# First layer's state recurrence: two half chains, or four quarter chains with products over half of K beside the last two

## The chip, the core and the metric

One core of a Trainium2 chip runs the whole program: two layers of a decoder on a sequence of 256 positions with 2048 channels. The metric is the time of one execution in microseconds (us) of device time. An instruction is put on one of five queues (TensorE, VectorE, ScalarE, GpSimd, and SyncE, which issues most DMAs), and each queue works through its own in order.

## What is computed

```python
def s5_mixer(u, ...):                      # first layer, u is the normed input
    ...                                    # lb = exp(lam*dt), coef = (lb-1)/lam, bb = coef*b
    st = scan(lb, u @ bb)                  # st[t] = lb*st[t-1] + bu[t], complex, 64 states a group
    y = st.re @ c.re - st.im @ c.im + d_skip * u
    val, gate = split(gelu(y) @ w_glu, 2)  # w_glu: 2048 x 4096
    return val * sigmoid(gate)

x = x + s5_mixer(rmsnorm(x))
x = x + swiglu_ffn(rmsnorm(x))
x = x + dilated_attention(...)             # second layer
x = x + swiglu_ffn(rmsnorm(x))
```

There are 128 groups of 16 channels, each with 64 complex states, and only this first layer has a recurrence. Everything else is a product with a large fp32 weight matrix.

## The kernel before

**Products.** Each weight matrix comes in chunks of 1 MB (four K tiles of 128 rows by 512 columns). ScalarE rounds half a chunk to `whi`, VectorE takes the rest into `wlo`, and TensorE multiplies them with activations that are split in the same way: three matmuls for each of two K tiles and two halves of the sequence, twelve for half a chunk. `products` (L113) issues them, `feed` (L127) a whole chunk, `block` (L146) a block of 512 output columns. Three buffers hold raw chunks, three hold `whi` and three `wlo`.

**The recurrence.** The 256 positions are cut into 64 blocks of four. The states are kept for 64 pairs of groups, as `sts`; a quarter `qr` has 16 of these pairs, so a quarter of the channels, and two quarters a half. For each quarter:

- `gain` and `taps` multiply the input matrix by the first three powers of lb (`gps`),
- `taps_T` transposes four pairs' worth of it, `inject` multiplies it with the input `ub` (built by `build_u`), and ScalarE copies the result into `sts`; sixteen such injections, four to a quarter,
- `scan` (L480) carries the state from block to block, 63 steps of three VectorE operations: a product with the fourth power into PSUM and two additions,
- `build_m` (L456) makes the matrix that acts inside a block, from `cp` (`build_c`) and `gps`; ScalarE copies it to `mt` and SyncE's queue shifts it by six small DMAs,
- `y_local` multiplies the inputs by `mt`, `y_state` the states by `fds` (`powers`), both into the same banks of PSUM; `gelu` follows, and `turn` and `low` transpose the result and split it into the activations `lhs` of the products.

In `s5_glu` the instructions of TensorE, ScalarE, GpSimd and, in part, VectorE keep the order in which they are written (`InOrder`), so this order is a schedule by hand. `run` takes one operation from each of several chains in turn, `steps` does so for a number of steps. Before the change there are two chains, `sa` for the first half of the pairs and `sb` for the second, with 128 and 64 elements to an operation. `sa` starts beside the taps of quarters 2 and 3, `sb` 16 steps behind it, and then both run side by side:

```python
        steps(LEAD - 6, sa)
        ...
        for qr in range(4):
            build_m(qr)
        ...
        steps(33 - LEAD, sa, sb)
        ...
        steps(16, sa, sb)
```

When `sa` is done, the first half's gelu and turn follow, then four half chunks of gate block 4 (over the first half of K, `high`, `rest` and `feed`) beside the last steps of `sb`, then the second half's `y_state` and gelu, then the other four half chunks. All other gate and value blocks come afterwards over the whole of K, with `block`.

GpSimd has `build_c`, `d_skip` and `powers`.

## Time and profile before

| | us |
|---|---|
| three runs of the kernel before | 2425.85, 2426.14, 2428.14 |
| their median | 2426.14 |
| span of the profiled execution, first to last instruction | 2426.5 |
| share of it in which TensorE is busy | 2391.7 |
| the same for VectorE, ScalarE, GpSimd | 1323.9, 1081.6, 113.5 |
| first 120 us of it: TensorE, VectorE | 90.4, 110.3 |

The execution that was profiled has no other time than its span, so the span stands for it. In the rows of the timeline there is the start, the time that a merged row is busy, the engine, the line, the operation, the tile written and those read, the shapes, and in brackets how long the engine was idle before it and who ended that. Inside `s5_glu` nearly every instruction has the line of `InOrder` (L59), so the tile names tell them apart: `mm<-mm,actr` and `actr<-actr,mm` are the recurrence, `ms<-dsm,ident` and `ms<-cb,gp` are build_m, `tr<-actr` and `ms<-actr` are y_local, `ms<-fdx,actr` and `tr<-fdx,actr` y_state, `gm` is gelu's result, `ms<-ident,gm` the turn, `actt` the activations.

### The profile page before, as it was taken

The page shows a single profiled execution, that of the slowest core. Times are in us where ns is not written, and L with a number is a line of the kernel's source. Part 1 is how long each engine was busy: PE and PEld are TensorE (multiplying, and loading weights), DVE is VectorE, ACT ScalarE, POOL GpSimd, SP SyncE. Part 2 cuts the span into 40 slices and gives each one's busy share as a digit, 9 for nine tenths or more (in the row PEclk, how much of TensorE's full clock was granted, in tenths as well). Part 3 has the DMA queues.
Part 4 walks back from the last instruction along what each step waited for, and adds up shares of the span by engine and source line. Part 5 has one row for each costly group of instructions (what it writes and reads, how often), then busy time and mean ns, then how long its engine had stood idle before and what let it go on. Part 6 is the DMA issues. An engine that isn't in the chain of part 4 may idle for free.

```text
span 2426.5 us, 29375 instructions
## 1 busy us (share of the span) xinstructions
PE 2391.7 (99%) x11856; PEld 1934.7 (80%) x11856; DVE 1323.9 (55%) x1974; ACT 1081.6 (45%) x1367; POOL 113.5 (5%) x113
## 2 busy tenths in 40 slices
PE   6899999999999999999999999999999999999999
PEld 5788888888888888888888888888888888888887
DVE  9955454444444454555446776765454444454454
ACT  7344444444334444554445555554444433344433
POOL 4800000000000000000000000000000000000000
PEclk9899999999999999999999999999999999999999
DMA  2245555555555555555554444445555555555554
GB/s 85 90 167 177 190 183 181 191 177 187 191 184 182 189 185 180 186 188 187 178 191 164 155 152 154 156 156 186 180 189 181 184 191 188 184 184 188 178 197 148
DMA packets 63033, 423.58 MB, mean 175 GB/s; under 512 B 8112, under 2 KB 9520, under 8 KB 12336
## 3 DMA queue, kind: packets, MB, share of 16 engines
q1 hardware_dynamic: 61744, 419.60, 50.8%
q8 instruction: 93, 1.52, 0.3%
q10 hardware_dynamic: 1152, 2.10, 0.2%
q14 instruction: 44, 0.36, 0.0%
HBM read 418.79 MB, written 2.10 MB: 173 GB/s over the span
## 4 chain that ended last, share of the span: by engine, by line
PE 97%; DVE 2%; ACT 1%; issue 0%; DMA 0%; SPq 0%; DVEq 0%
PE mm L122 30%; PE mm L124 30%; PE mm L123 30%; PE ms L59 2%; PE tr L59 1%; PE ms L863 1%; PE tr L743 1%; PE mm L59 1%; PE tr L814 1%; DVE mm L59 0%; PE tr L863 0%; PE tr L185 0%; DVE gp L59 0%; DVE gpb L59 0%; PE ms L893 0%
## 5 line engine op out<-in xcount | busy, mean ns | idle before, releaser
L104 DVE TENSOR_TENSOR wlo<-raw,whi 128x1024 fp32r<-128x1024 f32 x776 | 948.6, 1224 | 1001.5 <-ACT whi L103 1000.0
L103 ACT CAST whi<-raw 128x1024 fp32r<-128x1024 f32 x776 | 813.6, 1049 | 1159.4 <-PE mm L124 1139.7
L122 PE MATMUL mm<-whi,actt 128*128 128x512 f32 x3104 | 1234.8, 398 | 0.3 <-ACT whi L103 0.3
L124 PE MATMUL mm<-whi,actt 128*128 128x512 f32 x3104 | 1228.6, 396 | 0.0
L123 PE MATMUL mm<-wlo,actt 128*128 128x512 f32 x3104 | 1228.5, 396 | 0.0
L124 PEld LDWEIGHTS mm<-whi,actt 128*128 128x128 f32 x3104 | 582.6, 188 | 139.8
L123 PEld LDWEIGHTS mm<-wlo,actt 128*128 128x128 f32 x3104 | 582.6, 188 | 137.6 <-DVE wlo L104 0.4
L122 PEld LDWEIGHTS mm<-whi,actt 128*128 128x128 f32 x3104 | 582.6, 188 | 137.4 <-ACT whi L103 0.5
L794 POOL TENSOR_TENSOR sc<-ssq,mhalf 128x8 f32<-128x8 f32 x16 | 32.1, 2005 | 474.9 <-DVE ssq L792 474.9
L174 POOL TENSOR_TENSOR r<-m,mhalf 128x1 f32<-128x1 f32 x6 | 3.2, 552 | 1053.1 <-DVE m L173 846.4
L59 DVE TENSOR_TENSOR actr<-actr,mm 128x64 f32<-128x64 f32 x252 | 46.8, 216 | 2.0
L729 ACT ACTIVATE sg<-mm,r 128x512 f32<-128x512 f32 x44 | 30.1, 688 | 21.3 <-PE mm L124 21.0
L872 ACT ACTIVATE s<-s,mx 128x384 f32<-128x384 f32 (+1 forms) x32 | 24.8, 774 | 29.1 <-DVE mx L870 29.1
L59 DVE TENSOR_TENSOR mm<-mm,actr 128x128 f32<-128x128 f32 x126 | 37.0, 294 | 0.9
L59 POOL TENSOR_TENSOR fpr<-pf,cp 128x512 f32<-128x512 f32 x32 | 34.9, 1090 | 0.0
L733 DVE SCALAR_TENSOR_TENSOR sg<-mm,r,sg 128x512 f32<-128x512 f32 x44 | 30.9, 743 | 0.0
L59 ACT COPY actr<-ms 128x252 f32<-128x252 f32 (+1 forms) x40 | 19.8, 578 | 22.5 <-PE ms L59 21.2
L790 ACT ACTIVATE sq<-mm 128x512 f32<-128x512 f32 x32 | 19.0, 593 | 23.5 <-PE mm L124 23.5
L747 DVE TENSOR_TENSOR actt<-tr,actt 128x512 fp32r<-128x512 f32 x44 | 28.2, 682 | 0.0
L877 DVE SCALAR_TENSOR_TENSOR p<-s,z,p 128x128 f32<-128x128 f32 (+1 forms) x64 | 26.4, 412 | 3.2 <-ACT p L875 3.0
L746 ACT CAST actt<-tr 128x512 fp32r<-128x512 f32 x44 | 23.6, 590 | 10.0 <-PE tr L743 10.0
L743 PE MATMUL tr<-ident,sg 128*128 128x128 f32 x176 | 26.7, 274 | 0.0
(180 smaller groups left out, 938.0 us busy)
## 6 DMA issues: line engine op xcount, KB each, us to landing
raw<-w_gu SPq DMA_DIRECT2D x176, 1024.0 KB, 4.8
raw<-w_down SPq DMA_DIRECT2D x88, 1024.0 KB, 4.8
raw<-w_q SPq DMA_DIRECT2D x48, 1024.0 KB, 4.8
raw<-w_glu SPq DMA_DIRECT2D x32, 1024.0 KB, 4.8
raw<-w_kv SPq DMA_DIRECT2D x32, 1024.0 KB, 4.8
raw<-w_o SPq DMA_DIRECT2D x16, 1024.0 KB, 4.8
actr<-x_c SPq DMA_DIRECT2D x2, 1024.0 KB, 6.1
xr<-x_t SPq DMA_DIRECT2D x8, 256.0 KB, 5.2
```

The costliest lines, as they stand in the source:

```text
L59: return lambda *a, **k: self.tc.keep_in_program_order(call(*a, **k))
L103: (scalar or self.nc.scalar).copy(out=hi, in_=r)
L104: (vector or self.nc.vector).tensor_tensor(out=lo, in0=r, in1=hi.bitcast(FP32), op=ALU.subtract)
L122: matmul(ps[th], lhsT=a[:, 0, ts], rhs=hi, start=(k == 0), stop=False)
L123: matmul(ps[th], lhsT=a[:, 0, ts], rhs=lo, start=False, stop=False)
L124: matmul(ps[th], lhsT=a[:, 1, ts], rhs=hi, start=False, stop=(k == n - 1))
L729: nc.scalar.activation(out=s, in_=ps[th], func=AF.Silu, scale=rs[th])
L733: nc.vector.scalar_tensor_tensor(out=sg[th], in0=ps[th], scalar=rs[th], in1=sg[th], op0=ALU.mult, op1=ALU.mult)
L743: nc.tensor.transpose(out=pt[:, k, th * P:(th + 1) * P], in_=sg[th][:, c:c + P], identity=self.ident)
L747: nc.vector.tensor_tensor(out=ht[:, k0:k0 + 2, 1], in0=pt, in1=ht[:, k0:k0 + 2, 0].bitcast(FP32), op=ALU.subtract)
L794: nc.gpsimd.tensor_tensor(out=sc, in0=ssq, in1=self.mhalf.rearrange("p (a b) -> p a b", a=2), op=ALU.pow)
L877: nc.vector.scalar_tensor_tensor(out=pr, in0=sc[:, g], scalar=z, in1=pr, op0=ALU.mult, op1=ALU.add)
```

## The change

There are now four chains of one quarter each, with 64 and 32 elements to an operation. The first two, `sq[0]` and `sq[1]`, run side by side to their end. Then come the first half's gelu and turn, and then 28 half chunks of products over the first half of K, for seven of the eight gate and value blocks (`HALF1`). Between them VectorE takes two, two or three steps of `sq[2]` and `sq[3]` for each half chunk (`BSTEPS`). Six of the seven blocks are copied to SBUF by ScalarE as partial sums, since two pairs of PSUM banks serve them in turn; the seventh stays in PSUM. At the end of these products the second half's gelu and turn follow. Later each of the seven is fed over the other half of K (`whole`), and VectorE adds the partial sum. The twelve products of one half chunk (two K tiles) are called a slot in the prediction.

The same diff does more. The last quarter's taps and three of the four gains go to GpSimd. Taps have 512 elements to an operation instead of 256, nine operations instead of 18. The tables of lb's powers are written straight to PSUM, and ScalarE copies them to SBUF for GpSimd (`keep`). The coefficients are made right behind lb, den's operations before it. `pair` makes both parts of a complex product at once. The input `x_c` is loaded from ScalarE's queue instead of SyncE's, and the root mean square's scaling (`rc`) moves from VectorE to ScalarE. `y_local` for quarters 0 and 1 is written between the build_m of quarters 1, 2 and 3.

```diff
-LEAD = 16
+HALF1 = (0, 5, 1, 6, 2, 7, 4)
+BSTEPS = (2, 2, 3)
...
+        for q in range(2):
+            A.dma_start(out=xc[:, 16 * q:16 * q + 16], in_=io["x_c"][:, 16 * q:16 * q + 16])
...
+        def keep(t0, t1):
+            for t in range(t0, t1):
+                A.copy(out=pf[:, t].rearrange("p k r m -> p r k m"), in_=tabs[t])
...
-        def scan(h):
-            st = sts[h]
-            f, pr = fsc[h], prs[h]
+        def scan(qr):
+            st = sts[qr // 2][:, qr % 2]
+            f, pr = fsc[qr], prs[qr]
             for c in range(63):
                 hh, v = st[:, c], st[:, c + 1]
-                yield lambda: tt(pr, f, hh.unsqueeze(1).broadcast_to([P, 2, 2, 32]), ALU.mult, W)
+                yield lambda: tt(pr, f, hh.unsqueeze(1).broadcast_to([P, 2, 2, 16]), ALU.mult, W)
...
+        coefs()
         power()
-        gain(0)
         power()
...
+        gain(0, W)
+        for qr in (1, 3, 2):
+            gain(qr, G)
+        run(taps(0))
...
+        keep(0, 3)
+        build_c(0)
+        build_c(1)
+        run(taps(3, G))
+        d_skip()
         run(taps(1))
         power()
...
+        for i in range(4):
+            g0, gtt = gtt, taps_T(i + 1)
+            inject(i, g0)
+            if i == 0:
+                keep(3, 4)
...
+        sq = [scan(qr) for qr in range(4)]
+        run(itertools.islice(sq[0], 9), taps(2))
...
+        build_m(0)
+        build_m(1)
+        steps(32, sq[0], sq[1])
+        yl = {0: y_local(0, self.ps_tr, "tr")}
+        build_m(2)
+        yl[1] = y_local(1, self.ps_mm, "mm")
+        build_m(3)
...
+        for qr in range(2):
+            y_state(qr, yl[qr], 0, 32)
...
+        steps(28, sq[0], sq[1])
+
+        slots = [(b, c, h) for b in HALF1 for c in range(2) for h in range(2)]
...
+        def feed(k):
+            i, s = divmod(k, 4)
+            if s == 0:
+                self.blk = self.open_block(KT if i == last else KT // 2, 0, banks[i % 2])
+            r, hi, lo = ws.pop(k)
+            self.products(self.blk, [(hi[:, j], lo[:, j]) for j in range(2)], lhs, T)
+            if s == 3 and i < last:
...
+                part = room[i]
+                for th in range(2):
+                    A.copy(out=part[:, th], in_=self.blk[0][th])
+                parts[HALF1[i]] = [part[:, th] for th in range(2)]
...
+        high(0)
+        high(1)
+        y_state(0, yl[0], 32, 64)
+        gms[0] = gelu(yl[0])
+        steps(3, sq[1], sq[2])
+        rest(0)
+        y_state(1, yl[1], 32, 64)
+        pts = [turn(0, j4) for j4 in range(2)]
+        gms[1] = gelu(yl[1])
+        rest(1)
+        for j4 in range(2):
+            low(0, j4, pts[j4])
+        for k in range(len(slots)):
+            if k + 2 < len(slots):
+                high(k + 2)
+            if k > 0 and k + 1 < len(slots):
+                rest(k + 1)
+            if k < len(slots) - 2:
+                steps(BSTEPS[k % len(BSTEPS)], sq[2], sq[3])
+            feed(k)
+            if k == 0:
+                for j4 in range(2):
+                    low(1, j4, turn(1, j4))
+            if k == 3:
+                yl[2] = y_local(2, self.ps_ms, "ms")
+            if k == 17:
+                y_state(2, yl[2], 0, 32)
+            if k == len(slots) - 3:
+                y_state(2, yl[2], 32, 64)
+                gms[2] = gelu(yl[2])
+                run(sq[3])
+                yl[3] = y_local(3, self.ps_mm, "mm")
+                y_state(3, yl[3], 0, 64)
+                gms[3] = gelu(yl[3])
...
+                half = self.open_block(KT, KT // 2)
+                for c in range(2, 4):
+                    self.feed(half, src[c], lhs)
+                for th in range(2):
+                    nc.vector.tensor_tensor(out=parts[b][th], in0=half[0][th], in1=parts[b][th], op=ALU.add)
+                return parts[b]
```

Three places of the order of instructions follow. The first is TensorE between the last injections and the first turn; `gp` is the taps matrix of a quarter, `fdx` the output powers. Before:

```order
L59 MATMUL ms<-cb,gp_229 128x64 x16
L59 MATMUL ms<-dsm,ident 128x16x16 x2
L59 MATMUL ms<-cb,gp_230 128x64 x16
L59 MATMUL ms<-dsm,ident 128x16x16 x2
L59 MATMUL ms<-cb,gp_231 128x64 x16
L59 MATMUL ms<-actr 64x64 x32
L59 MATMUL tr<-actr 64x64 x32
L59 MATMUL ms<-fdx,actr 32x64 x64
L59 MATMUL tr<-fdx,actr 32x64 x64
L59 MATMUL mm<-actr 64x64 x32
L59 MATMUL mm<-actr 32x64 x64
L59 MATMUL ms<-fdx,actr 32x64 x64
```

And the same place of TensorE now:

```order
L60 MATMUL ms<-cb,gp_250 128x64 x16
L60 MATMUL tr<-actr 64x64 x32
L60 MATMUL ms<-dsm,ident 128x16x16 x2
L60 MATMUL ms<-cb,gp_251 128x64 x16
L60 MATMUL mm<-actr 64x64 x32
L60 MATMUL ms<-dsm,ident 128x16x16 x2
L60 MATMUL ms<-cb,gp_252 128x64 x16
L60 MATMUL tr<-fdx,actr 32x64 x64
L60 MATMUL mm<-fdx,actr 32x64 x64
L60 MATMUL tr<-fdx,actr 32x64 x64
L60 MATMUL mm<-fdx,actr 32x64 x64
L60 MATMUL ms<-ident,gm 128x128 x8
```

The two y_local have moved ahead of the build_m of quarters 2 and 3, and the third quarter's y_local and first y_state are gone from here.

The second place is VectorE where the first weights are split; `wlo<-raw,whi` is the low half of a slot's weights. Before:

```order
L59 TENSOR_TENSOR wlo<-raw,whi 128x1024
L59 TENSOR_TENSOR mm<-mm,actr 128x128
L59 TENSOR_TENSOR actr<-actr,mm 128x64 x2
L59 TENSOR_TENSOR mm<-mm,actr 128x128
L59 TENSOR_TENSOR actr<-actr,mm 128x64 x2
L59 TENSOR_TENSOR actt<-ms,actt 128x4x64 x4
```

And now, on VectorE:

```order
L60 TENSOR_TENSOR wlo<-raw,whi 128x1024 x2
L60 TENSOR_TENSOR actt<-ms,actt 128x4x64 x4
L60 TENSOR_TENSOR mm<-mm,actr 128x64 x2
L60 TENSOR_TENSOR actr<-actr,mm 128x32 x4
L60 TENSOR_TENSOR mm<-mm,actr 128x64 x2
L60 TENSOR_TENSOR actr<-actr,mm 128x32 x4
L60 TENSOR_TENSOR actt<-ms,actt 128x4x64 x4
L60 TENSOR_TENSOR wlo<-raw,whi 128x1024
```

A lone half chain has become a pair of quarter chains, with two products and four additions to a step, and the second turn's low half stands ahead of the third slot's split.

The third place is ScalarE around the first injections; `gt<-tr` copies transposed taps, `actr<-ms` copies an injection into the states. Before:

```order
L59 COPY gt<-tr 128x512 x2
L59 COPY actr<-ms 128x2x2x63 x2
L59 COPY gt<-tr 128x512
L59 COPY actr<-ms 128x2x2x63 x2
L59 COPY gt<-tr 128x512
```

And now, on ScalarE:

```order
L60 COPY pf<-mm 128x2x2x64 x3
L60 COPY gt<-tr 128x512 x2
L60 COPY actr<-ms 128x2x2x63 x2
L60 COPY pf<-mm 128x2x2x64
L60 COPY gt<-tr 128x512
L60 COPY actr<-ms 128x2x2x63 x2
```

The copy of the fourth power's table, which VectorE makes behind the second quarter's taps, stands between the first and the second injection.

More of the change, by code (lines that the diff above doesn't have):

```diff
@@ L352, in s5_glu, with coefs @@
-        prs = [half(tbq[:, 128:256]), half(tbp[:, 128:256])]
-        def gain(qr):
+            form(k, z)
+        cf = late.tile([P, 2, 2, 64], FP32, name="cform")
+        def coefs():
+            ni = lam[:, 1]
+            stt(t1, lam[:, 0], -1.0, ca, ALU.add, ALU.mult)
+            tt(t2, ni, cb_, ALU.mult)
+            stt(t3, lam[:, 0], -1.0, cb_, ALU.add, ALU.mult)
+            tt(t4, ni, ca, ALU.mult)
+            tt(cf[:, 0, 0], t1, t2, ALU.add)
+            tt(cf[:, 0, 1], t3, t4, ALU.subtract)
+            ts(cf[:, 1, 1], cf[:, 0, 0], -1.0, None, ALU.mult)
+            V.tensor_copy(out=cf[:, 1, 0], in_=cf[:, 0, 1])
@@ L506, in powers @@
             for t in range(4):
-                for k in range(2):
-                    pair(fds[qr][:, t, k], pf[t][:, :, k, mo:mo + 16], cp[:, :, mo:mo + 16])
+                pair(fds[qr][:, t], pf[:, t, :, :, mo:mo + 16], cp[:, :, mo:mo + 16])
         def y_local(qr, pool, nm):
@@ L607, in high, with rest @@
             A.copy(out=hi, in_=r)
-            ws[c, half] = (r, hi, lo)
-        def rest(c, half):
-            r, hi, lo = ws[c, half]
+            ws[k] = (r, hi, lo)
+        def rest(k):
+            r, hi, lo = ws[k]
             tt(lo, r, hi.bitcast(FP32), ALU.subtract, W)
-        def feed(c, half):
-            r, hi, lo = ws.pop((c, half))
-            self.products(gb0, [(hi[:, k], lo[:, k]) for k in range(2)], lhs, T)
-        gtile, lhs = {}, []
+        gtile = {}
         def turn(qr, j4):
@@ L638, in low @@
                 tt(lo, pt[:, :, xx], hi.bitcast(FP32), ALU.subtract, W)
-        def turns(qr):
-            for j4 in range(2):
-                low(qr, j4, turn(qr, j4))
-        high(0, 0)
-        high(0, 1)
-        high(1, 0)
-        y_state(0, yl[0], range(8), 32, 64)
-        gms = {0: gelu(yl[0])}
-        y_state(1, yl[1], range(4), 32, 64)
-        for half in range(2):
-            steps(3, sb)
-            rest(0, half)
-        steps(2, sb)
+        banks = [[t.rearrange("p a b c -> p (a b c)") for t in yl[qr]] for qr in range(2)]
@@ L662, in s5_glu @@
-        feed(0, 0)
-        high(1, 1)
-        pts = [turn(1, j4) for j4 in range(2)]
-        feed(0, 1)
-        steps(2, sb)
-        for j4 in range(2):
-            low(1, j4, pts[j4])
-        rest(1, 1)
-        run(sb)
-        feed(1, 0)
-        high(2, 0)
-        feed(1, 1)
-        rest(2, 0)
-        y_state(2, yl[2], range(8), 32, 64)
-        high(2, 1)
-        rest(2, 1)
-        gms[2] = gelu(yl[2])
-        yl[3] = y_local(3, self.ps_mm, "mm")
-        y_state(3, yl[3])
-        turns(2)
@@ L682, in s5_glu @@
-        gms[3] = gelu(yl[3])
-        feed(2, 0)
-        high(3, 0)
-        rest(3, 0)
-        feed(2, 1)
-        high(3, 1)
-        rest(3, 1)
-        turns(3)
-        feed(3, 0)
-        feed(3, 1)
+        for k in range(len(slots)):
[20 more added lines that the diff above has]
+                gms[3] = gelu(yl[3])
+            if k == len(slots) - 2:
+                pts = [turn(2, j4) for j4 in range(2)]
+            if k == len(slots) - 1:
+                for j4 in range(2):
+                    low(2, j4, pts[j4])
+                for j4 in range(2):
+                    low(3, j4, turn(3, j4))
@@ L692, in s5_glu @@
         late.release()
+        blk = self.blk
         with tc.tile_pool(name="glu", bufs=2, reuse_waits="tile") as work:
@@ L707, in s5_glu @@
                     sg.append(s)
-                ps = self.block([io["w_glu"][nb, c] for c in range(4)], lhs)
+                ps = whole(nb)
                 for th in range(2):
@@ L715, in s5_glu @@
                 self.xT_part(nb, nxt)
-            return [l for _, l in nxt], self.stats_end(), gains
+            res = [l for _, l in nxt], self.stats_end(), gains
+        carry.release()
+        return res
     def ffn(self, layer, lhs, rs, nxt=None, out=None):
```

248 lines of the change are left out of this document (113 added, 135 removed).

## Prediction

> **What bounds the kernel now.** I read the page first, then busy time by stage, then the timeline of the first 213 us.
>
> ```profile
> span 2426.5 us, 29375 instructions
> ...
> PE 97%; DVE 2%; ACT 1%; issue 0%; DMA 0%; SPq 0%; DVEq 0%
> ```
>
> The chain of work that ended last is TensorE's for 97% of the span. So the time is the products' own, plus whatever TensorE spends before and between them, and that lies in the first layer. The trace was taken on an execution with a span of 2426.5 us; the runs' median is 2426.14, so I sum on the trace and take the difference off the median.
>
> ```profile
> 60.10:75.10 15.00, 12.62 (x95) 11.29 (x95) 14.83 (x93) 7.38 (x18) 14.37 (x18) 1.00 0.08 22
> 75.10:92.20 17.10, 16.67 (x137) 15.50 (x138) 17.10 (x112) 4.65 (x10) 16.39 (x19) 0.50 0.29 90
> 92.20:119.00 26.80, 19.12 (x760) 17.83 (x756) 23.33 (x113) 7.41 (x15) 20.17 (x21) 0.87 0.34 111
> 131.20:157.00 25.80, 24.83 (x390) 20.57 (x390) 11.00 (x14) 10.69 (x21) 0.00 (x0) 1.00 0.26 89
> ```
>
> The columns are the stage, its length, busy time of PE, weight loads, VectorE, ScalarE and GpSimd, the granted clock and DMA. Up to 119 us VectorE is the full one in most stages: it runs the recurrence. TensorE waits for it, and from 75.1 to 92.2 it is busy at half clock.
>
> ```profile
> 119.01 0.50 PE L59 MATMUL tr<-whi,actt 128*128 128x512 f32 x1 [0.96 <-ACT gm L59]
> ...
> 157.42 0.39 PE L122 MATMUL mm<-whi,actt 128*128 128x512 f32 x1
> ...
> 158.12 0.40 PE L122 MATMUL mm<-whi,actt 128*128 128x512 f32 x1
> ```
>
> The first product starts at 119.0. Three products take 0.70 us, so a half chunk (12 products, from here on a slot) takes 2.80. By 157.0 the eight slots of the hand-written stage and a third of the next are done. From there TensorE runs dense, so 28 slots are done at 157.0 + 19.67 x 2.80 = **212.1 us** (the transposes of one x block, which the changed kernel still has to do at that point, are left out). What follows is the same work in both kernels; so the question is when the changed kernel has 28 slots done.
>
> **The change, part by part.**
>
> *Front of VectorE and the injections.* The tables, taps and injections come in another order.
>
> ```profile
> 2.77 0.70 DVE L290 COPY ldt<-spp 128x64 f32<-128x64 f32 x1 [2.77 <-DMA spp<-sp]
> ...
> 12.00 0.22 DVE L243 SCALAR_TENSOR_TENSOR lam<-t,mag 128x64 f32<-128x64 f32 x1
> ...
> 14.76 0.68 DVE L59 TENSOR_TENSOR gp<-bt,gb 128x512 f32<-128x512 f32 x1
> ```
> ```profile
> actr<-x_c SPq DMA_DIRECT2D x2, 1024.0 KB, 6.1
> ```
> ```profile
> 30.62 1.04 ACT L59 COPY actr<-ms 128x252 f32<-128x252 f32 x2
> ...
> 32.23 1.07 ACT L59 COPY actr<-ms 128x252 f32<-128x252 f32 x2
> ```
> ```profile
> 37.07 2.13 ACT L59 COPY actr<-ms 128x252 f32<-128x252 f32 x4
> ...
> 46.26 1.05 ACT L59 COPY actr<-ms 128x252 f32<-128x252 f32 x2 [1.59 <-PE ms L59]
> ```
>
> lam is ready at 12.2. The six added operations for den fill gaps of a dependent chain: 0.5. x_c now goes out on ScalarE's queue beside spp, for which VectorE's first operation waits: between nothing and the 3.3 by which x_c's 6.1 is above that 2.77; I take 1.0, since spp is small. From lam at 12.00 to the first gain at 14.76 stand one table, one power and rc's operation. A second power (about half of that, 1.3) and eight small operations for the coefficients (1.0) are added, and rc's goes to ScalarE: between 4.0 and 5.1, and I take 4.4. Then come a gain, 18 tap operations of 512 elements at 0.60 (by the line through 0.20 for 128 and 1.13 for 1024 elements, rows below), 12 waits of 0.13 on the operation before, and the third power: 0.6 + 10.8 + 1.6 + 1.3. That gives 12.2 + 0.5 + 1.0 + 4.4 + 14.3 = 32.4, and keep(3, 4), which ScalarE has in its row ahead of the next injections, ends at 32.8. Everything behind it on ScalarE waits: seven rounds of 1.61, less a transposed copy at the end, 10.7 to the eighth injection; 7.1 from there to the ninth's copies (39.2 to 46.26, with build_u between); then 1.05, five rounds (8.05), a copy (0.6) and the last injection on TensorE (1.1). **S**, where build_m starts, is 61.4, against 60.2 before. taps(3) leaves VectorE for GpSimd.
>
> ```profile
> L59 POOL TENSOR_TENSOR fpr<-pf,cp 128x512 f32<-128x512 f32 x32 | 34.9, 1090 | 0.0
> ```
>
> Nine of these are 10 us. From about 15, when the coefficients are there, GpSimd has three gains, two build_c (six operations) and taps(3): 18 x 1.09, done near 35. Their first reader is the thirteenth injection, near 54; with 19 us of cover the move costs nothing there, and VectorE is rid of 6 us. Behind it stand d_skip, powers(0), two build_c and powers(1), 32 operations more: near 70, and the first reader of powers(1) comes at 88 (below).
>
> *TensorE from S to the first product.*
>
> ```profile
> 60.16 1.10 PE L59 MATMUL ms<-dsm,ident 128*128 128x256 f32 x4
> 61.87 3.79 PE L59 MATMUL ms<-cb,gp 128*128 128x64 f32 x32 [0.60 <-ACT cb L59]
> 65.49 1.08 PE L59 MATMUL ms<-dsm,ident 128*128 128x256 f32 x4
> ...
> 71.05 1.08 PE L59 MATMUL ms<-dsm,ident 128*128 128x256 f32 x4
> ...
> 79.87 7.09 PE L59 MATMUL ms<-cb,gp 128*128 128x64 f32 x32
> 86.89 0.48 PE L59 MATMUL ms<-actr 128*64 128x64 f32 x4
> ```
> ```profile
> 91.06 2.59 PE L59 MATMUL tr<-actr 128*64 128x64 f32 x64
> 93.58 2.62 PE L59 MATMUL ms<-fdx,actr 64*32 64x64 f32 x126
> ```
> ```profile
> 131.28 9.73 PE L59 MATMUL mm<-actr 64*32 64x64 f32 x320
> ```
> ```profile
> 87.42 3.68 SPq L477 DMA_DIRECT2D actr<-actr  x6
> ```
> ```profile
> actr<-actr SPq DMA_DIRECT2D x8, 48.0 KB, 2.0
> ```
>
> At full clock the first two build_m take 5.33 and 5.56. y_local(0), now directly behind them, waits for the six shift copies of build_m(0) (issue 3.68, landing 2.0): about 1.0. It takes 2.6, and so does y_local(1); build_m(2) and (3) find their operands ready behind these, 4.9 each. Four half y_state at 2.65 are 10.6. Sum 37.5.
>
> ```profile
> 115.04 1.09 PE L59 MATMUL ms<-ident,gm 128*128 128x128 f32 x8
> 115.73 2.10 ACT L59 CAST actt<-ms 128x256 fp32r<-128x256 f32 x4 [0.47 <-PE ms L59]
> ...
> 116.89 2.24 DVE L59 TENSOR_TENSOR actt<-ms,actt 128x256 fp32r<-128x256 f32 x4 [2.68 <-ACT actt L59]
> ```
>
> From turn to the first low half are 2.4 us, in which two products already fit: 1.9. So the first product runs at S + 39.4 = **100.8 + h**, where h is what half clock costs. Here it cost 26.7 for four build_m (60.16 to 86.89) where the sum above has 20.7 to 22: about 5. Its bounds are 0 and, with all four build_m at 7.09 plus twice 1.08, 16 and more. I take 5, from the same work one rearrangement away. The Trainium skill's page TensorE: Matmul & The Clock Gate (Why this matters for your kernels) asks for an idle gap above about 3 us before the clock falls; by it h is 0. The trace disagrees: 16.67 of 17.10 us busy, clock 0.50.
>
> *VectorE: is the first half's recurrence ready by then?*
>
> ```profile
> 62.45 0.29 DVE L59 TENSOR_TENSOR mm<-mm,actr 128x128 f32<-128x128 f32 x1
> 62.65 0.35 DVE L59 TENSOR_TENSOR actr<-actr,mm 128x64 f32<-128x64 f32 x2
> 62.91 0.29 DVE L59 TENSOR_TENSOR mm<-mm,actr 128x128 f32<-128x128 f32 x1
> ```
> ```profile
> 53.38 0.30 DVE L59 TENSOR_TENSOR mm<-mm,actr 128x128 f32<-128x128 f32 x1
> 53.72 0.47 DVE L59 TENSOR_TENSOR actr<-actr,mm 128x64 f32<-128x64 f32 x2
> 54.23 0.30 DVE L59 TENSOR_TENSOR mm<-mm,actr 128x128 f32<-128x128 f32 x1
> ```
> ```profile
> 120.61 1.22 DVE L59 TENSOR_TENSOR wlo<-raw,whi 128x1024 fp32r<-128x1024 f32 x1
> 121.74 0.29 DVE L59 TENSOR_TENSOR mm<-mm,actr 128x128 f32<-128x128 f32 x1
> ```
>
> Two half chains side by side take 0.46 per step each, a lone one 0.85: 0.20 (128 elements) or 0.13 (64) until the next operation issues, 0.13 more until one that needs the result. A quarter's operations have 64 and 32 elements, 0.13 and 0.10. A pair's step is then 0.67 by issue and 0.72 by dependence: p = 0.73 (bounds 0.67, and 0.93 if size bought nothing). The scan starts when the fourth injection is in, three rounds behind 32.8, near 38. It runs 6.4 beside taps(2), and then 63 pair steps, 46: done at 90. TensorE asks at S + 34.8 = 96.2. Cover 6 us: the recurrence is off the path up to p = 0.82.
>
> *The loop.* 28 x 2.80 = 78.4. On TensorE between them: turn(1) 1.1, y_local(2) 2.6, y_state(2) 5.3, y_local(3) and y_state(3) 2.6 + 4.5 (9.73 less a local and a half state), turns 2.2, waits 0.5, and a wait at the third slot: VectorE splits its weights only after low(1), which ends some 2.9 behind turn(1) (115.04 + 1.09 to 116.89 + 2.24), so at 6.8 behind the first product, and the split at 8.0, where TensorE asks at 6.7; 1.2. In all 20.0. VectorE has 1.13 + 7/3 x 0.73 = 2.83 per slot against 2.80, hidden by the 7.9 of state work between. The partial sums (12 copies on ScalarE, 12 additions on VectorE) lie under products; they lengthen the way to three x blocks a little, 0.6. End: 100.8 + 98.4 + 0.6 = 199.8 + h. Against 212.1 the gain is 12.3 - h, so 7.3, and the forecast is **2419.0 us**.
>
> **Rivals.** *The clock stays full* (h = 0): 2413.8. For it: the new order is denser, and the two y_local break up the build_m. Against it: the row at 0.50. Chance 0.27; the clock page named above would give this one. *Small operations cost what large ones do* (p = 0.93): the first half's recurrence ends at 44.4 + 63 x 0.93 = 103, the first product is at 107.5 (a half y_state and 1.9 behind it), and in the loop VectorE needs 1.13 + 2.17 = 3.30 per slot. The tables in PSUM that y_local(3) overwrites are then free 8.0 + 24 x 1.13 + 58 x 0.93 + 2.5 = 91.5 behind the first product, where TensorE asks after 83.0 (26 slots are 72.8; turn(1), y_local(2), y_state(2) and the wait at the third slot are 10.2). So 107.5 + 98.4 + 8.5 + 0.6 = 215.0, or 2429. Against it: 0.20 and 0.13 for 128 and 64 elements. It eats the whole gain from p = 0.90 on. Chance 0.12. *Half clock from S to the first product*, the one on the slow side: four build_m at 9.25 are 16 more, the local and state products some 6 more, so 22 against a gain of 12.3: 2436. It decides from 17 us of loss on, which is nearly the whole stage of 39 us at half clock. For it: these matmuls did run at 0.50 while busy. Against it: in this stage the clock was back after 17.1 us. Chance 0.06. *Several small waits* that no row here shows eat most of the gain: 2424, chance 0.10. The DMA page of the Trainium skill (DMA: Bandwidth & Descriptors, Queues, rings and completion order) has engines take turns between queues by packet, which would make spp later than my 1.0; no run here shows it.
>
> **Numbers.** The forecast has 0.45. About 0.2% (4.9 us) can be told from no change. Faster: 0.40 of the forecast and the full clock, 0.67; slower: the half-clock rival and half of p = 0.93, with a remainder, 0.13; within, 0.20. Range 2412 to 2428: below it 0.04, above it 0.16.
>
> **What would show it.** Right: first product at 100 to 107, busy TensorE from build_m on, pair steps of 0.7 to 0.75, VectorE idle before the first product, 28 slots done by about 205. Wrong: TensorE waiting for VectorE ahead of y_state, wlo ahead of the products in most slots, or a clock of 0.50 over more than 17 us.

## The result, and the profile after

The changed kernel takes 2452.51 us (median of 4 runs, 2451.01 to 2453.20), the kernel before 2426.32 beside it: ratio 1.0107, 95% interval 1.0093 to 1.0122. It is 26 us slower, where 7.3 us faster was forecast, and lies outside the range. The profiled execution took 2451.01. One execution of a later kernel, e4_before_one, took 11396.57 and is left out of its time and ratio.

The page of the changed kernel: the span, and the chain of work that ended last.

```profile
span 2449.2 us, 29727 instructions
...
PE 91%; DVE 8%; issue 1%; ACT 0%; DMA 0%; DVEq 0%
...
L60 DVE TENSOR_TENSOR actr<-actr,mm 128x32 f32<-128x32 f32 x504 | 64.6, 184 | 8.0 <-ACT actr L60 3.5
L60 DVE TENSOR_TENSOR mm<-mm,actr 128x64 f32<-128x64 f32 x252 | 58.3, 231 | 8.1 <-ACT pf L60 0.4
```

Before, 97% of that chain was TensorE's; now 8% of it is VectorE's. The two groups are the recurrence. An operation on a quarter is hardly shorter than one on a half: 0.23 against 0.29 for a product, 0.18 against 0.22 for a sum, and there are twice as many.

TensorE's timeline ahead of the first product:

```profile
68.86 1.10 PE L60 MATMUL ms<-dsm,ident 128*128 128x256 f32 x4
...
98.53 1.64 PE L60 MATMUL mm<-fdx,actr 64*32 64x64 f32 x91 [1.80 <-issue]
114.77 3.45 PE L60 MATMUL tr<-fdx,actr 64*32 64x64 f32 x128 [14.60 <-DVE actr L60]
118.05 2.24 PE L60 MATMUL mm<-fdx,actr 64*32 64x64 f32 x128
...
121.58 0.50 PE L60 MATMUL tr<-whi,actt 128*128 128x512 f32 x1 [0.26 <-ACT actt L60]
```

TensorE has its first half states at 100.2 and then stands 14.60 us for the recurrence. This is VectorE in that wait, and later in the loop:

```profile
107.32 0.50 DVE L60 TENSOR_TENSOR mm<-mm,actr 128x64 f32<-128x64 f32 x2
107.85 0.51 DVE L60 TENSOR_TENSOR actr<-actr,mm 128x32 f32<-128x32 f32 x4
108.39 0.50 DVE L60 TENSOR_TENSOR mm<-mm,actr 128x64 f32<-128x64 f32 x2
...
128.97 1.22 DVE L60 TENSOR_TENSOR wlo<-raw,whi 128x1024 fp32r<-128x1024 f32 x1
...
132.14 1.22 DVE L60 TENSOR_TENSOR wlo<-raw,whi 128x1024 fp32r<-128x1024 f32 x1
...
136.38 1.22 DVE L60 TENSOR_TENSOR wlo<-raw,whi 128x1024 fp32r<-128x1024 f32 x1
```

Two products and four sums are a pair step: from 107.32 to 108.39 it is **1.07**, against the 0.73 of the forecast. GpSimd is idle by then. In the loop a slot with two pair steps takes VectorE 3.17 and one with three 4.24, so 3.53 on average, against TensorE's 2.80. Counted by the products' records, the 28th slot is done at 233.2, before at 213.1; that is 20.1 of the 22.7 by which the spans of the two traces differ.

### The profile page after: what moved, and what is told of

Its sections match the earlier page's. It is cut to its first block, busy times and chain, and to the rows that moved or that the text cites. A ratio compares the mean times of both kernels' runs of the same rounds, so it can differ in the third digit from the quotient of the medians.

```text
span 2449.2 us, 29727 instructions
## 1 busy us (share of the span) xinstructions
PE 2385.8 (97%) x11856; PEld 1925.3 (79%) x11856; DVE 1377.0 (56%) x2309; ACT 1088.8 (44%) x1384; POOL 122.7 (5%) x105
## 4 chain that ended last, share of the span: by engine, by line
PE 91%; DVE 8%; issue 1%; ACT 0%; DMA 0%; DVEq 0%
PE mm L123 29%; PE mm L124 29%; PE mm L125 29%; DVE mm L60 3%; DVE actr L60 2%; DVE wlo L60 1%; PE ms L898 1%; PE tr L778 1%; PE tr L849 1%; PE tr L898 0%; PE tr L186 0%; PE tr L60 0%; PE mm L60 0%; DVE gp L60 0%; PE ms L60 0%
## 5 line engine op out<-in xcount | busy, mean ns | idle before, releaser
L105 DVE TENSOR_TENSOR wlo<-raw,whi 128x1024 fp32r<-128x1024 f32 x756 | 924.3, 1224 | 967.2 <-ACT whi L104 965.8
L104 ACT CAST whi<-raw 128x1024 fp32r<-128x1024 f32 x756 | 792.8, 1049 | 1125.7 <-PE mm L125 1102.0
L123 PE MATMUL mm<-whi,actt 128*128 128x512 f32 x3008 | 1196.8, 398 | 0.0
L124 PE MATMUL mm<-wlo,actt 128*128 128x512 f32 x3008 | 1190.9, 396 | 0.0
L125 PE MATMUL mm<-whi,actt 128*128 128x512 f32 x3008 | 1190.8, 396 | 0.0
L125 PEld LDWEIGHTS mm<-whi,actt 128*128 128x128 f32 x3008 | 564.7, 188 | 135.1
L123 PEld LDWEIGHTS mm<-whi,actt 128*128 128x128 f32 x3008 | 564.7, 188 | 132.9
L124 PEld LDWEIGHTS mm<-wlo,actt 128*128 128x128 f32 x3008 | 564.7, 188 | 132.5
L60 DVE TENSOR_TENSOR actr<-actr,mm 128x32 f32<-128x32 f32 x504 | 64.6, 184 | 8.0 <-ACT actr L60 3.5
L60 DVE TENSOR_TENSOR mm<-mm,actr 128x64 f32<-128x64 f32 x252 | 58.3, 231 | 8.1 <-ACT pf L60 0.4
L60 ACT CAST whi<-raw 128x1024 fp32r<-128x1024 f32 x28 | 29.4, 1052 | 41.6 <-PE tr L60 21.0
L60 PE MATMUL tr<-whi,actt 128*128 128x512 f32 x128 | 42.1, 400 | 0.6 <-DVE actt L60 0.4
L60 DVE TENSOR_TENSOR wlo<-raw,whi 128x1024 fp32r<-128x1024 f32 x28 | 34.1, 1221 | 0.0
L60 PE MATMUL tr<-wlo,actt 128*128 128x512 f32 x64 | 26.3, 412 | 5.2 <-DVE wlo L60 4.6
L60 PE MATMUL mm<-whi,actt 128*128 128x512 f32 x96 | 30.7, 396 | 0.0
```

Of the source, the lines that this page charges most:

```text
L60: return lambda *a, **k: self.tc.keep_in_program_order(call(*a, **k))
L104: (scalar or self.nc.scalar).copy(out=hi, in_=r)
L105: (vector or self.nc.vector).tensor_tensor(out=lo, in0=r, in1=hi.bitcast(FP32), op=ALU.subtract)
L123: matmul(ps[th], lhsT=a[:, 0, ts], rhs=hi, start=(k == k0), stop=False)
L124: matmul(ps[th], lhsT=a[:, 0, ts], rhs=lo, start=False, stop=False)
L125: matmul(ps[th], lhsT=a[:, 1, ts], rhs=hi, start=False, stop=(k == n - 1))
```

## The experiments

Two questions: why the pair step takes 1.08 (theory A: the chains wait for each other; theory B: small operations are slow), and where the front lost its 7 us. All ratios are to the kernel before, run beside it; a range in brackets is the 95% interval.

**e1_apart.** The products of the two chains in different PSUM tiles, and the chains one operation apart.

```diff
...
-        prs = [half(tb2[:, 256 + 64 * k:320 + 64 * k], 16) for k in range(4)]
+        prs = [half((tb2, tb3)[k % 2][:, 256 + 64 * k:320 + 64 * k], 16) for k in range(4)]
...
-        run(itertools.islice(sq[0], 9), taps(2))
+        run(itertools.islice(sq[0], 10), taps(2))
...
+        run(itertools.islice(sq[2], 1))
         steps(3, sq[1], sq[2])
```

The lines left out here give tb3 room for these products and change nothing else.

> The changed kernel, with the products of the odd quarters' chains in another PSUM bank than those of the even ones, and the second chain of a pair one operation behind the first. In the changed kernel a pair step of two quarter chains took 1.08 us where 0.73 was forecast. Theory A (the pair is slow because its two products lie in one PSUM tile, so that each chain's product waits until the other chain has written or read its own): with two tiles only the waits inside a chain are left, 0.267 behind a product and 0.221 behind a sum, and by issue and dependence the pair step becomes 0.74. The first half's recurrence, which has some 60 pair steps from 50 us on, ends near 95 in place of 114.8, TensorE (done with the first half states at 100.2) no longer waits, the first product starts near 107, a half chunk costs VectorE 1.13 + 7/3 x 0.74 = 2.86, 28 slots are done near 206 in place of 233.2, and the time is near 2425. Theory B (operations of 64 and 32 elements are slow by themselves, by a fixed cost or because their factor is read in runs of 16): the pair step stays at 1.08 and the time within 3 us of 2452.5.

Measured 2427.94, ratio 1.0007 (0.9998 to 1.0016): 24.6 us come back. VectorE's timeline of this run, at the same work:

```profile
71.10 0.23 DVE L60 TENSOR_TENSOR mm<-mm,actr 128x64 f32<-128x64 f32 x1
71.24 0.31 DVE L60 TENSOR_TENSOR actr<-actr,mm 128x32 f32<-128x32 f32 x2
71.47 0.23 DVE L60 TENSOR_TENSOR mm<-mm,actr 128x64 f32<-128x64 f32 x1
71.60 0.32 DVE L60 TENSOR_TENSOR actr<-actr,mm 128x32 f32<-128x32 f32 x2
71.83 0.23 DVE L60 TENSOR_TENSOR mm<-mm,actr 128x64 f32<-128x64 f32 x1
```

From 71.10 to 71.83 is a pair step: 0.73, with operations of the same length as in the changed kernel (0.23 and 0.18). So it was not their size. The loop from first product to 28th slot takes 97.0 in place of 111.6. The first product starts at 117.0, though, not at 107, and TensorE's waits say why:

```profile
101.42 1.45 PE L60 MATMUL mm<-fdx,actr 64*32 64x64 f32 x82 [1.66 <-issue]
...
105.43 1.57 PE L60 MATMUL tr<-fdx,actr 64*32 64x64 f32 x88 [1.91 <-issue]
...
112.44 2.77 PE L60 MATMUL mm<-fdx,actr 64*32 64x64 f32 x91 [4.80 <-issue]
```

"issue" means that nothing that the profile shows was waited for: 8.4 us in the middle of the half state products. The changed kernel has only the first such wait (1.80); TensorE had the rest of this work behind the end of the recurrence. More on it below.

What made the chains wait stands in the built programs: VectorE's operations wait for a count of VectorE's own finished operations. In the changed kernel and in this one, A being the first chain of the pair:

```
changed          waits for  is      e1_apart         waits for  is
product A           683    684      product A           681    683
product B           684    685      second sum B        682    684
first sum A         685    686      first sum A         683    685
first sum B          -     687      product B           684    686
second sum A        686    688      second sum A        685    687
second sum B        687    689      first sum B         686    688
product A           689    690      product A           687    689
```

On the left product B waits for product A (684), the first sum of A for product B (685), and the next product A for the last sum of B (689): operations of the other chain, whose data they don't touch. What they share is the tile tb2, which holds all products: the program keeps its waits by tile. On the right each waits for the one two places back, which is its own chain's. With 0.035 from an end to a waiting start (two products: 0.50 less 0.23 is 0.27 from start to start), 0.23 and 0.186 for their lengths and 0.105 without a wait, the left column makes 0.267 + 0.267 + 0.221 + 0.105 + 0.221 = 1.08, the measured step.

**e4_before_one.** The reverse, in the kernel before: one tile for both half chains' products.

```diff
-        fsc = [half(tbp[:, 0:128]), half(tbq[:, 0:128])]
-        prs = [half(tbq[:, 128:256]), half(tbp[:, 128:256])]
+        fsc = [half(tbp[:, 0:128]), half(tbp[:, 128:256])]
+        prs = [half(tbq[:, 128:256]), half(tbq[:, 0:128])]
```

> The kernel before, with the products of its two half chains in one PSUM tile and their two factor tables in another, everything else as it was; the operations keep their 128 and 64 elements. Theory A (chains that share a tile wait for each other): a pair step of two half chains goes from 0.93 to about 1.42 (each half of it: 0.33 behind a product, 0.13 for the next sum, 0.25 behind that one); of 47 pair steps before the first product most lie on the path, so the first product comes at 137 to 142 in place of 119.0 and the time is 2444 to 2449. Theory B (small operations are slow by themselves): nothing changes, 2426 within 3 us.

Measured 2448.66 (median of three), ratio 1.0090 (1.0073 to 1.0107), with the operations' sizes untouched.

```profile
70.58 0.30 DVE L59 TENSOR_TENSOR mm<-mm,actr 128x128 f32<-128x128 f32 x1
70.91 0.35 DVE L59 TENSOR_TENSOR actr<-actr,mm 128x64 f32<-128x64 f32 x2
...
72.02 0.30 DVE L59 TENSOR_TENSOR mm<-mm,actr 128x128 f32<-128x128 f32 x1
```

70.58 to 72.02 are two products and a step of both chains: 1.44 (0.93 before), and the first product comes at 137.9. Theory B is out.

**e11_banks and e12_offset.** The two halves of e1_apart apart: e11_banks has the two tiles alone, e12_offset the two lines that set the chains one operation apart.

> The changed kernel with the two PSUM tiles alone, without the offset between the chains. The kernel with both edits took 0.73 for a pair step, the changed one 1.08. Theory A (the waits between the chains set the step) can be counted out: an operation starts 0.035 behind the end of the one it waits for (0.232 for a product, 0.186 for a sum), else 0.133 or 0.100 behind the start of the one before. With two tiles and no offset the second product still waits for the first, which reads the factors in its tile, and the step comes to 0.84. The first half's recurrence is then done near 101, as TensorE's half states, and the first product hardly moves against the kernel with the offset (117); in the loop VectorE needs 1.13 + 7/3 x 0.84 = 3.09 per slot against 2.80, less the 7.9 of state work between and 3 more for the last local product: 2429 to 2433. Theory B (a tile is slow when two chains use it, whatever the order): 0.73, as with the offset, and the time 2428.

> The changed kernel with the offset alone: the second chain one operation behind the first, both with their products in one PSUM tile. By the same count each chain's product waits for the other's sum and the next sum for that product, and the step goes up from 1.08 to 1.13, so the time to about 2455. If it is the distance between the chains that counts and not the tile, it falls towards 0.73 and the time towards 2428.

Measured 2433.13, ratio 1.0019 (1.0008 to 1.0030), and, in a single execution of e12_offset, 2466.28. In e11_banks a pair step takes 0.86 (0.84 by the count), in e12_offset 1.18 (1.13):

```profile
69.91 0.49 DVE L60 TENSOR_TENSOR mm<-mm,actr 128x64 f32<-128x64 f32 x2
70.31 0.53 DVE L60 TENSOR_TENSOR actr<-actr,mm 128x32 f32<-128x32 f32 x4
70.77 0.49 DVE L60 TENSOR_TENSOR mm<-mm,actr 128x64 f32<-128x64 f32 x2
```
```profile
69.89 0.23 DVE L60 TENSOR_TENSOR mm<-mm,actr 128x64 f32<-128x64 f32 x1
...
71.07 0.23 DVE L60 TENSOR_TENSOR mm<-mm,actr 128x64 f32<-128x64 f32 x1
```

The order of the four kernels is that of their waits: 0.73, 0.86, 1.08, 1.18, and times of 2428, 2433, 2453, 2466. The offset helps with two tiles and hurts with one. (e12_offset lies 11 us above its forecast, which was added up too low: against the changed kernel its step is 0.10 longer, and on 126 pair steps that is 12.6 of the 13.8 between the two times.) These runs do not vary the tile apart from the place in PSUM that it stands for; against a slower PSUM speaks that the operations have the same lengths in all four, 0.23 and 0.18, and that the counted waits alone give 0.74, 0.84, 1.08 and 1.13, each within 0.05 of the measured step.

**e2_front.** Now the front. In the changed kernel, VectorE's and GpSimd's timelines side by side:

```profile
14.64 0.22 DVE L245 SCALAR_TENSOR_TENSOR lam<-t,mag 128x64 f32<-128x64 f32 x1
14.77 1.30 DVE L248 TENSOR_TENSOR t<-lam,cb__224 128x64 f32<-128x64 f32 x1
...
16.13 1.18 DVE L245 SCALAR_TENSOR_TENSOR t<-lam,ca 128x64 f32<-128x64 f32 x1
...
17.37 1.19 DVE L245 SCALAR_TENSOR_TENSOR t<-lam,cb__224 128x64 f32<-128x64 f32 x1
...
18.61 0.21 DVE L248 TENSOR_TENSOR t<-lam,ca 128x64 f32<-128x64 f32 x1
...
22.07 0.87 DVE L60 TENSOR_TENSOR pw<-pr 128x128 f32<-128x128 f32 x1
...
23.89 1.59 DVE L60 TENSOR_TENSOR gp<-bt,gb 128x512 f32<-128x512 f32 x1
```
```profile
14.66 3.82 POOL L60 TENSOR_TENSOR gp<-bt,gb 128x512 f32<-128x512 f32 x3
```

Three operations of 64 elements last until GpSimd's three gains end, one each; the fourth, behind them, takes 0.21. GpSimd was kept idle there:

```diff
-        coefs()
         power()
         power()
         gain(0, W)
-        for qr in (1, 3, 2):
-            gain(qr, G)
         run(taps(0))
+        gain(1, W)
+        coefs()
...
         build_c(1)
+        for qr in (2, 3):
+            gain(qr, G)
         run(taps(3, G))
```

> The changed kernel, with GpSimd kept idle until the first tap products are done: the gain of the second quarter goes back to VectorE, the coefficients are made behind the first taps, and GpSimd's two gains stand behind its first two build_c. In the changed kernel three coefficient operations beside GpSimd's gains took 1.2 to 1.3 us in place of 0.22, two power sums beside build_c 0.70 and 0.87 in place of 0.29, and the first gain 1.59 in place of 0.68. Theory A (a VectorE operation with both operands in SBUF stands until the GpSimd operation beside it is through): these operations fall back to 0.22, 0.29 and 0.68, the third power ends near 36 in place of 39.7, and as the first half's recurrence is what TensorE waits for, the first product moves up by about as much, to 118: near 2449. Theory B (they were late for another reason, a table or a transfer that they waited for): the third power ends no earlier than 39, and the time is within 1 us of 2452.5, or up to 1.5 later for the gain that VectorE has again.

Measured 2452.33, ratio 1.0102 (1.0085 to 1.0119): no gain. The scheduler put the coefficients back ahead of the powers, so GpSimd started at 16.4 and stalled other operations; the three coefficient operations fell to 0.22, the third power ended 2.4 earlier (37.3), but build_m began only 0.8 earlier (68.0). The windows of the three rounds of injections behind that power say where the rest went, in e2_front and then in the changed kernel (in the order of the columns shown before, the clock and the DMA share stand ahead of the last):

```profile
38.20:43.00 4.80, 4.78 (x40) 3.71 (x40) 0.42 (x1) 3.41 (x8) 4.72 (x4) 0.64 0.00 0
```
```profile
40.60:45.40 4.80, 4.80 (x60) 3.81 (x60) 1.29 (x5) 4.61 (x11) 4.72 (x4) 1.00 0.00 2
```

In 4.8 us TensorE did 40 matmuls at a clock of 0.64 in e2_front, 60 at 1.00 in the changed kernel: two rounds against three. Ahead of these rounds it had stood idle longer, 3.99 against 2.63. The first product came at 120.9, 0.7 earlier, and that was lost too: at the end of the loop TensorE has a wait that the changed kernel does not have, and its 28 slots are done at 235.6, 2.4 later than there. The three rows are e2_front, the changed kernel, and e2_front again:

```profile
38.22 1.39 PE L60 MATMUL ms<-actr,gt 128*64 128x128 f32 x16 [3.99 <-ACT gt L60]
```
```profile
40.60 1.09 PE L60 MATMUL ms<-actr,gt 128*64 128x128 f32 x16 [2.63 <-ACT gt L60]
```
```profile
226.54 1.51 PE L60 MATMUL mm<-actr 64*64 64x64 f32 x40 [1.60 <-issue]
```

The local theory holds; the step "and as the first half's recurrence is what TensorE waits for, the first product moves up by about as much" fell.

**e8_pr_psum and e5_sbuf** test the sharing by itself: an operand of the power's sum goes to PSUM, and an operand of the odd chain's sums to SBUF.

```diff
-            pr = early.tile([P, 2, 2, 64], FP32, name="pr")
-            tt(pr, tabs[0], pw[-1].unsqueeze(1).broadcast_to([P, 2, 2, 64]), ALU.mult, W)
-            tt(z, pr[:, :, 0], pr[:, :, 1], ALU.add, W)
+            pr = early.tile([P, 2, 64], FP32, name="pr")
+            pa = tb3[:, 256:384].rearrange("p (k m) -> p k m", k=2)
+            for r, d in enumerate((pr, pa)):
+                tt(d, tabs[0][:, :, r], pw[-1][:, r].unsqueeze(1).broadcast_to([P, 2, 64]), ALU.mult, W)
+            tt(z, pa, pr, ALU.add, W)
```

> The changed kernel, with the two products of a power in two operations, one of them written to PSUM, so that the sum behind them has one operand there and the other in SBUF; GpSimd's work beside it is the same. Theory A (it is two SBUF operands beside GpSimd that make an operation stand): the first two sums, 0.70 and 0.87 in the changed kernel, take 0.20 to 0.30, and the first gain, which still has both operands in SBUF, stays near 1.6 or falls between 0.7 and 1.6 by where in GpSimd's operation it starts. Theory B (the sum waits for its table or is slow by its place in the program): 0.7 to 0.9 as before. The time hardly moves, within 2 us of 2452.

A single execution took 2452.18. The two sums take 0.29 each, beside the same GpSimd operations; the gain behind them, with both operands in SBUF, still waits (1.36 against 0.68 in the kernel before).

```profile
19.36 0.29 DVE L60 TENSOR_TENSOR pw<-mm,pr 128x128 f32<-128x128 f32 x1
...
21.26 0.29 DVE L60 TENSOR_TENSOR pw<-mm,pr 128x128 f32<-128x128 f32 x1
...
22.51 1.36 DVE L60 TENSOR_TENSOR gp<-bt,gb 128x512 f32<-128x512 f32 x1
```

```diff
-        prs = [half(tb2[:, 256 + 64 * k:320 + 64 * k], 16) for k in range(4)]
+        prs = [half(tb2[:, 256 + 64 * k:320 + 64 * k] if k % 2 == 0 else ds[:, k // 2], 16) for k in range(4)]
```

> The changed kernel, with the products of the odd quarters' chains in SBUF (in the space of the skip coefficients, free by then), those of the even ones in PSUM as before, and no offset between the chains. The two tiles are apart, as in the run with two PSUM banks, so the waits between the chains are gone; but the two sums of the odd chain now have both operands in SBUF, while GpSimd works 9.6 of every 10 us up to 104. Theory A (such an operation stands until GpSimd's is through): each of the two sums meets a GpSimd operation of 1.06 to 1.27, a pair step takes about 2.2 us up to the end of GpSimd's work near 105, 25 of 60 are done by then, the other 35 take 0.72 each, the first product starts near 137, and with a loop that runs at TensorE's rate the time is 2448 to 2457. Theory B (no sharing between the two engines; the slow operations of the front had another cause): the pair step is 0.71 throughout, and the time is that of the run with two banks, 2428.

Measured 2448.09, ratio 1.0093 (1.0079 to 1.0107), at the lower edge of theory A's range and 20 from theory B's. While GpSimd works, then behind it:

```profile
69.44 0.90 DVE L60 TENSOR_TENSOR actr<-actr,ds 128x32 f32<-128x32 f32 x1
70.26 0.17 DVE L60 TENSOR_TENSOR actr<-actr,mm 128x32 f32<-128x32 f32 x1
70.37 1.10 DVE L60 TENSOR_TENSOR actr<-actr,ds 128x32 f32<-128x32 f32 x1
```
```profile
119.65 0.22 DVE L60 TENSOR_TENSOR mm<-mm,actr 128x64 f32<-128x64 f32 x1
...
120.03 0.19 DVE L60 TENSOR_TENSOR actr<-actr,ds 128x32 f32<-128x32 f32 x1
...
120.37 0.23 DVE L60 TENSOR_TENSOR mm<-mm,actr 128x64 f32<-128x64 f32 x1
```

The sum with its product in SBUF takes 0.90 and 1.10 beside GpSimd, the one with it in PSUM 0.17, and behind GpSimd's work both are alike and the pair step is 0.72. The Trainium skill's page SBUF — State Buffer (Who interferes with whom) says just this: a VectorE operation with two SBUF inputs and a GpSimd operation that reads SBUF exclude each other, one input in PSUM frees it. The traces agree (0.17 against 1.10).

**e3_both.** Both edits, and x_c's loads on SyncE's queue behind spp and pairs.

```diff
-        for q in range(2):
-            A.dma_start(out=xc[:, 16 * q:16 * q + 16], in_=io["x_c"][:, 16 * q:16 * q + 16])
...
         nc.sync.dma_start(out=pairs, in_=io["pairs"])
+        for q in range(2):
+            nc.sync.dma_start(out=xc[:, 16 * q:16 * q + 16], in_=io["x_c"][:, 16 * q:16 * q + 16])
```

> The two edits before together, and x_c back on SyncE's queue behind spp and pairs. If spp is late because x_c's transfers share the DMA engines with it, VectorE starts at 2.8 in place of 5.4. If all three theories hold, the third power ends near 33.5, build_m starts near 63, the recurrence is done near 90, before TensorE's first half states (near 94.5), the first product starts near 101, 28 slots are done near 200, and the time is near 2417, below the kernel before. If the pair step stays at 1.08, the recurrence is done near 108 and the time is 2444 to 2447. If x_c's queue makes no difference to spp, 2419.

Measured 2423.22, ratio 0.9985 (0.9976 to 0.9994): faster than both kernels, by 2.8 us against the one before, less than forecast. spp lands as before the change, at 2.62:

```profile
2.62 0.85 DVE L295 COPY ldt<-spp 128x64 f32<-128x64 f32 x1 [2.62 <-DMA spp<-sp]
```

build_m starts at 63.3, where 63 was expected, and the recurrence is done at 92.7, ahead of TensorE, but the first product starts at 106.5, not at 101: three waits for "issue" again, 1.81, 1.65 and 3.69. The executions of this one kernel run from 2420.97 at a granted clock of 0.997 to 2426.40 at 0.994, a wider spread than the gain.

**e6_xt, e9_all, e10_loads, e13_loads2** followed those waits. Each ends 1.0 to 1.6 behind the end of a 16 KB transfer of the instruction queue, which suggests that TensorE's code was late; no row names what it waited for. e6_xt issues x_t's loads from the loop.

```diff
+            if 9 <= k < 17:
+                if k == 9:
+                    self.alloc_x()
+                th, nb = divmod(k - 9, 4)
+                A.dma_start(out=self.x[th][nb], in_=io["x_t"][th][:, nb * 512:(nb + 1) * 512])
...
-                    nc.sync.dma_start(out=self.x[th][nb], in_=io["x_t"][th][:, nb * 512:(nb + 1) * 512])
```

> The kernel with both edits and x_c on SyncE's queue, and the eight loads of x_t (2 MB) issued from ScalarE's queue, one behind each of the slots 9 to 16, where in that kernel they start at 98.8. There TensorE stood 1.81, 1.65 and 3.69 us in the half state products (93.3, 97.0 and 102.9), each time until 1.0 to 1.9 behind the end of a 16 KB transfer of the instruction queue; the third such transfer started at 100.6, with the DMA engines full. Theory A (TensorE's code comes late where loads fill the DMA engines): the third wait falls to about that of the two others, 1.7, the first product starts near 104.5 and the time is near 2421.2. Theory B (the waits are those of the products, for results or weights): all three stay and the time is 2423 within 1. Either way the waits of 1.7 stay, with the second and third weight chunk in flight.

Measured 2425.89, ratio 0.9998 (0.9989 to 1.0007); the third wait is 3.99. x_t is not its cause. The time itself says little here: build_m starts at 66.7, 3.3 later than in e3_both and before any of the loads that were moved. e9_all is e6_xt with e8_pr_psum's edit:

> The kernel with both edits, x_c on SyncE's queue and x_t late, and with one product of each power in PSUM. If all that the runs so far say holds, the second power is done about 1 us earlier, build_m starts near 62.5, and the time is 2420.5, 1 below the run with x_t late alone and 5.5 below the kernel before. If the power sums are not freed, or the injections behind them give the microsecond back to the clock, it is that of the run with x_t late.

Measured 2425.60, ratio 0.9994 (0.9985 to 1.0003): no difference from e6_xt that shows. Then the second and third weight chunk were issued later, from ScalarE, behind one pair of gelus each, and (e13_loads2) both behind the second pair:

```diff
...
+        def later(k):
+            b, c, h = slots[k]
+            raws[b, c] = self.wraw.tile([P, 4, 512], FP32, name="raw")
+            A.dma_start(out=raws[b, c], in_=io["w_glu"][b, c])
...
         gms[0] = gelu(yl[0])
+        later(2)
...
         gms[1] = gelu(yl[1])
+        later(4)
```

> The kernel with x_t late, and its second and third weight chunk (1 MB each) loaded from ScalarE's queue, behind the first and behind the second pair of gelus, where in that kernel both start at 96.2 and fill the DMA engines from 99 to 105.3. There the third wait of TensorE in the half state products was still 3.99, so x_t had not made it: the 16 KB transfer of the instruction queue that ends it started at 103.4, 6.3 behind the one before, where the others follow each other at 3.5. Theory A (code comes late behind whatever loads fill the DMA engines, here the two chunks): that transfer starts near 100.7, the wait falls to about 1.4, like the two others, and the first product comes some 2.5 earlier in relation to build_m, 2425.9 less 2.5 or 2423.4, the clock being equal; if the second chunk is then late for the third slot, TensorE waits there for its split and up to 3 of it is lost again. Theory B (the wait belongs to the place in TensorE's code): 4.0 stays, whatever is in flight.

> As the run before with the two chunks from ScalarE's queue, but both behind the second pair of gelus. In that run the first of them went out at 100.2 and filled the DMA engines from 100 to 104, and the third transfer of TensorE's code fell into just that stretch (102.1 to 103.0), so it told the theories not apart. Now no load is in flight between the first chunk and the end of the half state products. Theory A (code comes late behind loads that fill the DMA engines): the third wait falls from 3.96 to 1.4 to 1.8, the first product comes 2.4 earlier in relation to build_m, and the time is near 2422, or up to 3 later if the second chunk is late for the third slot. Theory B (the wait belongs to the place in TensorE's code): 4.0 stays with idle DMA engines.

Measured 2424.18, ratio 0.9983 (0.9974 to 0.9992), and 2426.44, ratio 0.9999 (0.9990 to 1.0007). TensorE in e10_loads, then in e13_loads2:

```profile
104.57 2.77 PE L60 MATMUL mm<-fdx,actr 64*32 64x64 f32 x91 [3.96 <-issue]
```
```profile
105.55 2.75 PE L60 MATMUL mm<-fdx,actr 64*32 64x64 f32 x91 [3.42 <-issue]
...
120.70 0.50 PE L60 MATMUL tr<-wlo,actt 128*128 128x512 f32 x1 [3.10 <-DVE wlo L60]
```

The wait hardly moves, and e13_loads2 pays 3.10 for its late second chunk. But no run had the DMA engines idle throughout. In e13_loads2 SyncE issued its next chunk at 99.0, once the first one's buffer was free:

```profile
99.02 24.66 SPq L97 DMA_DIRECT2D raw<-w_glu  x2
```
```profile
100.00:102.00 2.00, 2.00 (x128) 1.99 (x128) 0.00 (x0) 0.43 (x2) 1.92 (x2) 1.00 0.96 303
```

By the window's row the DMA engines were 0.96 busy from 100 to 102, and the third transfer of code began at 103.2, when they came free. What delays it stays open, and so does how much the loads have to do with it.

## Why the prediction was wrong

It named the right place, VectorE's recurrence, and the right limit: "off the path up to p = 0.82". The step that failed is **p = 0.73**, which was 1.08. It took the time until the next operation issues and the dependence inside each chain, and left out waits between the chains. The bounds (0.67, and 0.93 if size bought nothing) were read from rows of two half chains whose products lie in two tiles; the change puts all products into tb2, which the diff shows, and nothing in the sum asked who else waits on that tile. The number itself was right only for chains in two tiles and one operation apart: e1_apart has 0.73, e11_banks without the offset 0.86, beyond the limit of 0.82. Even e1_apart's 2427.94 is 9 above the forecast; the front and TensorE's waits for "issue" are the other terms, below. (The last sum is also off by 0.2: 2426.14 less 7.3 is 2418.8.) Of the 30.0 us between forecast and trace (-7.3 against +22.7):

| step | forecast | measured |
|---|---|---|
| S, start of build_m | 61.4 | 68.9 |
| recurrence of the first half done | 90 | 114.8 |
| first product | 105.8 (h = 5) | 121.6 |
| first product to the end of 28 slots, later terms included | 99.0 | 111.6 + 1.6 |
| one x block behind slot 28, left out | 0 | 0.9 |

That is 15.8 + 14.2 + 0.9, less 1.0 since the kernel before had its 28 slots at 213.1, not 212.1: 29.9.

- **The front, 32.4 to the third power:** 39.7. spp cost 2.6 in place of 1.0, inside its bounds. The Trainium skill's page DMA: Bandwidth & Descriptors (Queues, rings and completion order), by which queues take turns by packet, pointed there, and spp at 5.4 beside x_c and at 2.62 ahead of it agrees. From lam to the first gain 9.25 in place of 4.4, and that gain 1.6 in place of 0.6: the stalls beside GpSimd, and forms that go to one PSUM tile one behind the other (0.26 each, 0.10 before in SBUF). The 18 tap operations took what was forecast.
- **"The move costs nothing there"** looked at who waits for GpSimd and not at who works beside it. taps(3) was done at 39.7, early enough, and taps(1) beside it kept its 0.70, with an operand in PSUM. It was the gains and build_c beside the coefficients and powers. The Trainium skill's page SBUF — State Buffer (Who interferes with whom), which the prediction did not weigh, speaks against just this.
- **TensorE from S:** h was 0 in this trace (granted clock 1.00 from 68.9 to 100.2, 31.3 to the half states); that rival's premise held, and what it gave was covered by the recurrence. The sum lacked the waits for "issue": 6.3 to 8.4 where nothing covers them. The kernel before has them too, 4.67 at 101.7 and 1.56 at 113.3.
- **The loop:** 2.83 per slot against 2.80 became 3.53, hidden no longer. With p back at 0.73 it takes 97.0, near the 98.4.
- **The partial sums' 0.6** were nothing; the 1.6 above is the last transposes, which stand behind slot 28.
- **The rival with p = 0.93** had the place and the side, at a chance of 0.12, and for the wrong reason: e4_before_one and e1_apart show that size was not it. Its price, 2429, is near where e11_banks (0.86, 2433) lies.

Shown: the waits in the chains (five kernels, both directions), the sharing of VectorE and GpSimd (three kernels). Argued only: how much of the front's 7.5 us each of its parts cost the end, since e2_front gave none of it back; and that the waits for "issue" are waits for code.

## What to carry to other kernels

Two chains that are interleaved to hide each other's latency lose much of that if they write to one PSUM tile of a program that keeps its waits by tile: give each its own, and count the waits in the built program, not the data flow, before pricing a step. When work moves to GpSimd, ask what VectorE does beside it with both operands in SBUF. And when one wait of 15 us is removed, look for what stood in its shadow: here 6 to 8 us of it were other waits of TensorE, by all signs for its own code.

## What the runs showed of the hardware

- A VectorE operation with two SBUF operands lasted as long as GpSimd's beside it (0.22 became 1.18 to 1.30); with one in PSUM it was not touched (0.87 became 0.29).
- Products of 64 elements took 0.23 and sums of 32 took 0.18, where twice the size took 0.29 and 0.22: most of a small operation is not its elements.
- In bursts of small TensorE instructions (128 matmuls with their weight loads in 2.3 us) 16 KB came on the instruction queue about once per burst. Where the recurrence did not cover it, TensorE stood 1.4 to 4.8 us in three of the four bursts and went on 1.0 to 1.6 us behind the end of such a transfer.
